# A hybrid state-space and attention layer on one core: other steps for the state-space units inside the attention loop

## The chip, the core and the metric

One NeuronCore of one Trainium2 chip runs the whole layer in one launch. Its engines are TensorE (matrix products, "PE" in the profile, "PEld" for its weight loads), VectorE ("DVE"), ScalarE ("ACT"), GpSimd ("POOL") and SyncE ("SP", which here only issues DMAs). Products are written to PSUM banks, and ScalarE and VectorE read them from there. The metric is device time in microseconds, median of the runs.

## The reference

For 2048 tokens of width 1024, one layer of a hybrid trunk, in float32:

```python
h = rmsnorm(x, norm_mix_g)
proj = h @ w_in
u_ssm, q, k, v = ...                      # 512 columns each
y_ssm = s5_mixer(u_ssm, ...)              # diagonal complex state-space layer, 32 groups of 16, GELU and a GLU
y_att = chunked_attention(q, k, v, rel_bias)   # 8 heads of 64; own chunk of 64 frames and 8 chunks before it
mixed = concatenate([rmsnorm(y_ssm, g1), rmsnorm(y_att, g2)])
x = x + mixed @ w_out
h2 = rmsnorm(x, norm_ffn_g)
x = x + (silu(h2 @ w_gate) * (h2 @ w_up)) @ w_down
return rmsnorm(x, norm_final_g)
```

The state-space layer is a recurrence over time with a constant complex factor per state: `s[t] = a * s[t-1] + B u[t]`, `y[t] = Re(C s[t]) + D u[t]`.

## The kernel before

**Stages.** First the columns of the state-space input are projected (`u_phase`), then comes the attention stage (`att_phase`), in which the rest of the projection, attention and the state-space recurrence are interleaved; then the mixing and output projection (`mix_phase`), the gated feed-forward (`gate_up_phase`) and the down projection (`down_phase`). Products are written in parts of high and low precision, so that one product of two operands is three matmuls (`mm3`).

**The attention loop.** `att_phase` goes through 128 steps: 4 blocks of 512 tokens, in each 4 pairs of heads, 2 heads, 4 groups of 128 queries. One step writes, in the order given by `ORDER` ("s", "p", "t", "f"): the scores of this step (tile `sc`, PSUM, one buffer; VectorE adds the bias and takes the minimum `mn`, L963, ScalarE takes the exponential, L966), then at the end of a head the product with the values (`pv_head`, or `pv_scale` one step later, both in PSUM tile `pj`, two buffers), then the transposes of the probabilities of two steps before (tile `pt`, PSUM, one buffer; ScalarE copies the high part `pth`, L982, and VectorE the low part `ptl`, L983), and last "f": a share of the filler work. At the steps whose number is 24 or 25 in a block (24, 25, 56, 57, 88, 89) the order is "p", "t", "f", "s". Here step n begins in the trace with its `sc` products; what the text calls f(n) is the filler work of step n, so f(88) stands ahead of the scores of step 88, and f(79) behind step 79's and directly ahead of step 80's.

**The filler work** is a list of `Unit` objects: a generator, a number n of parts, a first step s0 and an end step s1, and `pre`. `Unit.advance(s)` is called for each unit of the list, in the order of the list, at each step. From step s0 - pre on it runs the first part (the loads). From s0 on it runs so many parts that they are spread evenly up to s1; `mid=(m, ...)` asks for one part more from step s0 - m on. The projections of q, k and v of the next block (tile `pf`) and its hidden state (`hT_unit`: scaled by VectorE, L793, split in a high part by ScalarE, L813, and a low part by VectorE, L815) are in the list first. A block change is at steps 24, 56 and 88: there the last projection of one block ends and the first of the next one begins (`CUT[0]` is -8 and `CUT[-1]` is 24).

**The state-space units.** At the end of the list stand, for b = 0 to 7, `ssm_front(b)` and then `ssm_back(b)`, so that within a step the back of unit b comes ahead of the front of unit b + 1. The text counts them from one: the first unit is b = 0, the seventh b = 6.

- `ssm_front`: one part that loads the input `U` (for the second unit, b = 1, into two tiles that attention has left free) and the matrix `Bst` (L606); then two parts, one for each half q of the unit's groups: products with `Bst` into a `pj` bank and four ScalarE copies into tile `X` (L630); then 22 parts in which GpSimd scans over time (L644 to L647, then L655 and L656), and at the end issues four DMAs that carry the states from `X` to tile `XG` (L678). Each instruction of the scan works on both halves of `X`. `X`, `XG`, `Bst`, `Tm` and `Vm` have one buffer each.
- `ssm_back`: loads `Tm` (L687) and `Vm` (L692); then for each half q two products with `Tm` and `U` and two with `Vm` and `XG` into a `pj` bank, which ScalarE copies back to `U` (L701); then a store of `U` to `y` (L703).

TensorE's instructions keep the order in which the program writes them (`k.ta` and `k.te` pin every matmul). On the other engines the framework that builds the kernel chooses the order within what the data allow.

**Where the units stand** (lines 709 to 711, and line 1066, one long line):

```python
ST = 2, 10
SX = 4, 19, 33, 45, 56, 68, 80, 92
SY = 20, 34, 46, 57, 69, 81, 93, 105
...
units.append(Unit(ssm_front(...), SSM_F, SX[b], SX[b] + 9, SX[b] - 2 if b == 0 else 4, light=SL))
units.append(Unit(ssm_back(k, sp, psum, S, b), SSM_B, SY[b], SY[b] + 2, 6, light=SL))
```

`SSM_F` is 25 parts over 9 steps: at step SX[b] the front runs both halves and the first step of the scan. `SSM_B` is 4 parts over 2 steps: at step SY[b] the back runs both halves. So, from the second unit on, each back stands one step behind the front of the next unit: fronts at 33, 45, 56, 68, 80, 92 and backs of the unit before at 34, 46, 57, 69, 81, 93.

## Time and profile before

| | |
|---|---|
| median of 3 runs | 2189.12 us (2188.07 to 2189.96) |
| profiled execution, its time | 2187.64 us |
| its span in the trace | 2185.5 us |
| TensorE busy | 2144.4 us, 98% of the span |
| VectorE, ScalarE, GpSimd busy | 1535.0, 1008.2, 378.7 us |
| attention steps 0 to 127, first scores to last | 126.3 to 665.5 us |
| scores of step 21, 46, 47 | from 208.7, 309.7, 319.4 us |
| scores of step 69, 79, 80 | from 415.0, 458.0, 460.6 us |
| scores of step 88, 92 | from 499.7, 519.1 us |

The time of an execution holds some 2 us beside the span of the trace. In the rows below the first number is the start of an instruction (or of a merged run of equal ones, "x8") in us from the span's start, the second its duration; in square brackets stands how long the engine was idle before it and what released it. In a table of windows the columns are the window, its length, the busy time of each engine with its number of instructions, the granted TensorE clock as a share of full speed (PEclk), the busy share of the DMA engines and GB/s. Matmul durations overlap, so the pace of TensorE is read from one start to the next.

### The profile page before, as it was taken

What the parts mean: (1) busy time and instruction counts of PE and PEld (TensorE: products, weight loads), DVE (VectorE), ACT (ScalarE), POOL (GpSimd) and SP (SyncE); (2) the same over time, 40 slices, a digit from 0 to 9 for tenths busy, and PEclk for the clock granted to TensorE, in tenths of its full rate; (3) what the DMA queues carried; (4) which work ended last, traced back from release to release, by engine and by line L of the source; (5) the groups of instructions that cost most, each with busy time, mean ns of one, the idle gap of its engine ahead of it and who ended that gap; (6) DMA issues with size and microseconds to landing.
All of it is one profiled execution on the core that took longest, in us unless ns stands there. A gap on an engine that the chain in (4) does not pass through costs nothing.

```text
span 2185.5 us, 30150 instructions
## 1 busy us (share of the span) xinstructions
PE 2144.4 (98%) x10606; PEld 1810.5 (83%) x10606; DVE 1535.0 (70%) x2680; ACT 1008.2 (46%) x1697; POOL 378.7 (17%) x849
## 2 busy tenths in 40 slices
PE   8998999999998999999999999999999999999998
PEld 7787898898887888888888888888888888888887
DVE  8767566666567667766776769766665587688785
ACT  7356466555586621533333345333333443353322
POOL 3367777676310000000000000000000100000000
PEclk9999999999999999999999999999999999999999
DMA  9788877965745346834554757555433476575552
GB/s 337 229 285 266 295 231 247 306 218 167 211 145 178 111 144 206 286 108 148 173 184 139 246 197 278 189 174 193 158 124 98 153 291 221 192 252 182 202 212 78
DMA packets 197592, 440.12 MB, mean 201 GB/s; under 512 B 20225, under 2 KB 37681, under 8 KB 190337
## 3 DMA queue, kind: packets, MB, share of 16 engines
q1 hardware_dynamic: 188816, 410.34, 56.1%
q0 software_dynamic: 8624, 27.86, 4.1%
q8 instruction: 83, 1.36, 0.3%
q14 instruction: 69, 0.56, 0.1%
HBM read 294.72 MB, written 135.29 MB: 197 GB/s over the span
## 4 chain that ended last, share of the span: by engine, by line
PE 89%; DVE 5%; DMA 2%; ACT 2%; issue 2%; SPq 0%; POOL 0%; DVEq 0%; ACTq 0%
PE X L83 22%; PE ps L83 22%; PE Y L83 11%; PE pf L83 10%; PE big L83 9%; PE W L83 5%; PE pj L83 4%; PE pt L86 2%; PE sc L83 2%; DVE ptl L983 1%; DVE w L182 1%; DVE lo L815 0%; DMA w<-wss 0%; DMA xt<-in_xp 0%; PE pp L83 0%
## 5 line engine op out<-in xcount | busy, mean ns | idle before, releaser
L83 PE MATMUL X<-hi,c 128*128 128x512 f32 x1408 | 448.9, 389 | 0.0
L83 PE MATMUL ps<-hd,hd 128*128 128x512 f32 (+1 forms) x1920 | 428.0, 384 | 0.0
L83 PEld LDWEIGHTS ps<-hd,hd 128*128 128x128 f32 x1920 | 353.4, 188 | 70.9 <-DVE hd L182 0.3
L83 PEld LDWEIGHTS X<-hi,c 128*128 128x128 f32 x1408 | 264.3, 188 | 55.2 <-DVE c L182 0.4
L83 PE MATMUL X<-lo,c 128*128 128x512 f32 x704 | 273.9, 389 | 0.0
L182 ACT CAST hd<-hd 128x1536 fp32r<-128x1536 f32 (+2 forms) x114 | 148.0, 1309 | 226.3 <-DMA hd<-hq 165.1
L83 PE MATMUL Y<-hi,c 128*128 128x512 f32 x696 | 222.2, 389 | 0.0
L182 DVE TENSOR_TENSOR hd<-hd 128x1536 fp32r<-128x1536 f32 (+2 forms) x114 | 174.8, 1539 | 32.3 <-ACT hd L182 31.9
L182 DVE TENSOR_TENSOR c<-S,c 128x512 fp32r<-128x512 f32 x175 | 120.2, 687 | 98.7 <-ACT c L182 98.4
L1620 ACT COPY u<-X 128x512 f32<-128x512 f32 x132 | 77.5, 587 | 191.6 <-PE X L83 191.5
L83 PE MATMUL big<-m,woh 128*128 128x512 f32 x512 | 160.1, 394 | 0.0
L1830 DVE TENSOR_TENSOR acc<-acc,ps 128x512 f32<-128x512 f32 x196 | 130.4, 681 | 42.1 <-PE ps L83 41.7
L182 ACT CAST c<-S 128x512 fp32r<-128x512 f32 x175 | 108.6, 622 | 107.5 <-PE Y L83 58.0
L83 PEld LDWEIGHTS X<-lo,c 128*128 128x128 f32 x704 | 132.2, 188 | 27.3
L83 PEld LDWEIGHTS Y<-hi,c 128*128 128x128 f32 x696 | 130.7, 188 | 27.3 <-DVE u L1624 0.2
L182 ACT CAST c<-raw 128x512 fp32r<-128x512 f32 x130 | 81.0, 623 | 152.2 <-PE Y L83 72.0
L83 PE MATMUL pf<-hi,w 128*128 128x512 f32 x416 | 148.2, 409 | 0.0
L1808 POOL DMA_DIRECT2D hd<-hq x4 | 2.5, 628 | 810.9 <-PE X L83 810.1
L83 PE MATMUL Y<-lo,c 128*128 128x512 f32 x348 | 135.4, 389 | 0.0
L983 DVE TENSOR_TENSOR ptl<-pt,pth 128x640 fp32r<-128x640 f32 (+3 forms) x152 | 98.1, 645 | 45.1 <-ACT pth L982 41.2
L966 ACT ACTIVATE s<-s,mn 128x640 f32<-128x640 f32 (+4 forms) x128 | 97.9, 765 | 50.7 <-DVE mn L963 47.8
L982 ACT CAST pth<-pt 128x640 fp32r<-128x640 f32 (+3 forms) x152 | 83.8, 551 | 76.3 <-PE pt L86 70.8
(514 smaller groups left out, 4280.6 us busy)
## 6 DMA issues: line engine op xcount, KB each, us to landing
w<-wss SPq DMA_DIRECT2D x36, 1024.0 KB, 6.9
hq<-g SPq DMA_DIRECT2D x140, 256.0 KB, 2.1
hd<-hq SPq DMA_DIRECT2D x35, 768.0 KB, 4.4
hd<-wc SPq DMA_DIRECT2D x35, 768.0 KB, 5.9
raw<-in_w_up SPq DMA_DIRECT2D x44, 512.0 KB, 4.0
raw<-in_w_gate SPq DMA_DIRECT2D x43, 512.0 KB, 3.7
wc<-px SPq DMA_DIRECT2D x66, 256.0 KB, 3.0
wss<-w SPq DMA_DIRECT2D x12, 1024.0 KB, 6.6
```

The lines of the kernel that those rows point to most:

```text
L83: return self.tc.keep_in_program_order(self.tc.nc.tensor.matmul(*a, **b))
L86: return self.tc.keep_in_program_order(self.tc.nc.tensor.transpose(*a, **b))
L182: return nc.scalar.copy(hi, raw), nc.vector.tensor_tensor(lo, raw, f32(hi), op=ALU.subtract)
L966: nc.scalar.activation(s[:, :nk], s[:, :nk], AF.Exp, bias=mn[:], scale=-1.0, accum_out=sums[sb, pr][:, hh, qp : qp + 1])
L982: k.high = nc.scalar.copy(pth[:, a:b, qp, :], pt[:, a:b, :]).ins
L983: k.low = nc.vector.tensor_tensor(ptl[:, a:b, qp, :], pt[:, a:b, :], f32(pth[:, a:b, qp, :]), op=ALU.subtract).ins
L1620: self.kept = nc.scalar.copy(u[:], ps[:]).ins
L1808: k.ahead = nc.gpsimd.dma_start(f32(lo[:, d]), src[d].rearrange("g p c -> p g c")).ins
L1830: V.tensor_tensor(a, a, ps[:], op=ALU.add)
```

## The change

```diff
 ST = 2, 10
-SX = 4, 19, 33, 45, 56, 68, 80, 92
-SY = 20, 34, 46, 57, 69, 81, 93, 105
+SX = 4, 19, 33, 45, 56, 67, 78, 92
+SY = 24, 34, 46, 57, 68, 79, 88, 105
+SPRE = SX[0] - 2, 9, 4, 4, 4, 4, 4, 4
...
-                units.append(Unit(qk_unit(sb, 0), QK_N, g0 + C[0], g0 + C[1], 3, light=LIGHT))
+                units.append(Unit(qk_unit(sb, 0), QK_N, g0 + C[0], g0 + C[1], 5 if sb == 1 else 3, light=LIGHT))
...
-            units.append(Unit(ssm_front(...), SSM_F, SX[b], SX[b] + 9, SX[b] - 2 if b == 0 else 4, light=SL))
+            units.append(Unit(ssm_front(...), SSM_F, SX[b] + 1, SX[b] + 9, SPRE[b] + 1, light=SL, mid=(1,)))
```

What it does:

1. **Front in two steps, for all eight units.** With `s0 = SX[b] + 1` and `mid=(1,)` the front's first half (products and four copies) is written at step SX[b], and the second half at step SX[b] + 1, where the scan begins. The scan still ends at step SX[b] + 8.
2. **Fronts sooner.** The sixth unit (b = 5) from step 68 to 67, the seventh (b = 6) from 80 to 78; their loads, four steps ahead, move with them.
3. **Backs moved.** The first unit from step 20 to 24 and the seventh from 93 to 88, both block changes; the fifth from 69 to 68 and the sixth from 81 to 79, so that they stay one step behind the next front. Their loads, six steps ahead, move with them.
4. **Two loads sooner.** The inputs of the second unit's front are loaded from step 10 instead of 15 (`SPRE[1]` is 9), and the weights of the second block's first q and k projection (`qk_unit(1, 0)`) from step 19 instead of 21.

## The prediction

> **What bounds the kernel now.** I read the page first: busy shares, slices, chain.

> ```profile
> PE 2144.4 (98%) x10606; PEld 1810.5 (83%) x10606; DVE 1535.0 (70%) x2680; ACT 1008.2 (46%) x1697; POOL 378.7 (17%) x849
> ...
> PE 89%; DVE 5%; DMA 2%; ACT 2%; issue 2%; SPq 0%; POOL 0%; DVEq 0%; ACTq 0%
> ```

> TensorE carries the time. The change leaves its products as they are, so it can win only pauses of TensorE and stretches with a low clock, and lose only by new ones. Next come TensorE's waits in the loop (120 to 590 us) and a table of windows around two block changes.

> ```profile
> engine line waited for: us in total, times, longest us
> PE pt L86 <- DVE ptl L983: 7.4, 10, 1.3
> PE sc L83 <- DVE mn L963: 6.6, 6, 1.9
> ...
> 195.70:232.10 36.40, 32.56 (x155) 26.10 (x154) 25.55 (x56) 21.27 (x57) 24.70 (x53) 0.95 0.87 288
> 498.00:520.00 22.00, 17.61 (x91) 14.73 (x90) 16.48 (x25) 11.09 (x21) 9.61 (x11) 0.92 0.77 238
> ```

> TensorE mostly waits for VectorE. Around the first block change (195.7 to 232.1) it idles 36.40 - 32.56 = 3.84 us, and the clock of 0.95 costs 0.05 x 36.4 = 1.8 us more: 5.7 us to win at most. Around the third it is 22.00 - 17.61 = 4.4 us and 0.08 x 22 = 1.8 us: 6.2 us. Nothing else that the change touches has as much to give.

> **First block change: back of the first unit from f(20) to f(24), second unit's loads sooner.** Here are VectorE's pauses (three rows) and TensorE's rows behind them.

> ```profile
> 203.24 0.29 DVE L963 CUSTOM_DVE_ANT_0 s<-sc,nbb 128x128 f32<-128x128 f32 x1 [4.16 <-PE sc L83]
> ...
> 206.12 0.29 DVE L983 TENSOR_TENSOR ptl<-pt,pth 128x128 fp32r<-128x128 f32 x1 [1.26 <-ACT pth L982]
> ...
> 209.36 0.43 DVE L963 CUSTOM_DVE_ANT_0 s<-sc,nbb 128x256 f32<-128x256 f32 x1 [1.14 <-PE sc L83]
> ```

> ```profile
> 201.06 1.10 PE L83 MATMUL pj<-hi0x,Bst 128*128 128x256 f32 x4 [1.32 <-DMA Bst<-bsts]
> ...
> 205.47 0.59 PE L83 MATMUL pj<-U,Tm 128*128 128x256 f32 x2
> 205.90 0.59 PE L83 MATMUL pj<-XG,Vm 128*128 128x256 f32 x2
> ...
> 208.73 0.47 PE L83 MATMUL sc<-k,q2h 128*128 128x256 f32 x1
> ```

> TensorE first waits 1.32 us for `Bst`, then spends 208.73 - 205.47 = 3.3 us on the back, and VectorE, fed by it, idles 4.16 + 1.26 + 1.14 = 6.6 us; afterwards it is late with its splits, and TensorE waits for it. With the loads five steps sooner the first wait goes, hidden under projection work; if SP's queue held them back again it would cost the same 1.3 us. The back at f(24) fills the pauses there instead of starving VectorE at f(20). The gain lies between 1.3 us (the load alone) and 5.7 us (all of it). VectorE's 6.6 us of idle time exceed the loss, but its work in the stretch is dense afterwards, so I take **-4.5 us**, nearer to the upper end. Splitting the copies (eight of 0.38 us, row below) into two fours shortens ScalarE's longest block by 1.5 us and fills a pause elsewhere: at nothing, within 0.5 us. The sooner weights of the second block's first q and k shift an SP issue by two steps; no wait for them stands in the rows: nothing.

> **What the split does to the scan.** The second half of a front is now written in the step of the previous unit's back, and behind it in the list. The scan needs both halves. From the second unit's back on, its start therefore moves behind that back. And `XG` must land before the back's `Vm` products, which stand in TensorE's fixed order: whatever is behind them (scores, transposes, everything) waits. So I follow the chain: second half ready, copies, scan, four DMAs, landing.

> ```profile
> 464.99 3.03 ACT L630 COPY X<-pj 64x256 f32<-64x256 f32 x8 [1.54 <-issue]
> ...
> 468.10 0.48 POOL L644 TENSOR_TENSOR st<-X,a 128x128 f32<-128x128 f32 x1 [9.27 <-ACT X L630]
> ```

> ```profile
> L678 POOL DMA_DIRECT2D XG<-X x4: 602/617/632, 501.9 to 507.6; - x4
> ...
> DMA to landing us min/median/max: 3.6/4.0/4.8
> ```

> These are the seventh unit: the scan takes 507.6 - 468.10 = 39.5 us to its fourth DMA, which lands some 4.0 us later. Ahead of it stand four copies (4 x 0.38 = 1.5) and the end of the product (0.25). The whole chain is 1.75 + 39.5 + 4.0 = **45.3 us** from the end of f(SX + 1). The fourth and sixth unit:

> ```profile
> 312.42 0.50 POOL L644 TENSOR_TENSOR st<-X,a 128x128 f32<-128x128 f32 x1 [10.46 <-ACT X L630]
> ...
> L678 POOL DMA_DIRECT2D XG<-X x4: 599/618/635, 345.9 to 351.3; - x4
> ...
> DMA to landing us min/median/max: 2.4/3.8/4.4
> ```

> ```profile
> 417.71 0.49 POOL L644 TENSOR_TENSOR st<-X,a 128x128 f32<-128x128 f32 x1 [17.15 <-ACT X L630]
> ...
> L678 POOL DMA_DIRECT2D XG<-X x4: 599/616/632, 452.9 to 458.2; - x4
> ...
> DMA to landing us min/median/max: 2.3/2.9/3.4
> ```

> That is 1.75 + 38.9 + 3.8 = 44.4 and 1.75 + 40.5 + 2.9 = 45.1 us. Against it stands TensorE's own time between the same points:

> ```profile
> 319.44 0.50 PE L83 MATMUL sc<-k,q2h 128*128 128x320 f32 x1
> ...
> 361.09 0.59 PE L83 MATMUL pj<-U,Tm 128*128 128x256 f32 x2
> ...
> 364.36 0.50 PE L83 MATMUL sc<-k,q2h 128*128 128x320 f32 x1
> ...
> 413.49 1.89 PE L83 MATMUL pj<-U,Bst 128*128 128x256 f32 x8
> 415.02 0.50 PE L83 MATMUL sc<-k,q2h 128*128 128x320 f32 x1
> ...
> 460.60 0.31 PE L83 MATMUL sc<-k,q2h 128*128 128x320 f32 x1
> ...
> 463.88 1.89 PE L83 MATMUL pj<-rsn,Bst 128*128 128x256 f32 x8
> 465.42 0.50 PE L83 MATMUL sc<-k,q2h 128*128 128x320 f32 x1
> ...
> 499.73 0.31 PE L83 MATMUL sc<-k,q2h 128*128 128x320 f32 x1
> ```

> A front's products take 465.42 - 463.88 = 1.5 us, half of them 0.75.
> - *Back of the fourth unit, f(57).* From the end of f(46) (319.44) to its first product (361.09) it is 41.65 us; half a front moves behind it, -0.75; its second group, which needs the fourth DMA, comes 2 x 0.43 us later (205.47 to 205.90): 41.8. Chain 44.4: a wait of 2.6. The next front's first copies may not write `X` before the DMAs have read it, and they hold one of two `pj` banks that the back's second half wants: 1.5 us of copies against 0.4 of products left, 1.1 more. **+3.7** (with landings from 2.4 up to 8.4, below: 1.2 to 8.3).
> - *Back of the sixth, f(79).* From 415.02 to 460.60 it is 45.6 us; the fifth unit's back now lies ahead, -3.3, half a front lies inside, +0.75, the two groups +0.85: 43.9. Chain 45.1: 1.2, and 1.1 for the bank. **+2.3** (0 to 7.8).
> - *Back of the seventh, f(88).* From 460.60 to 499.73 it is 39.1 us; without the front (-1.5) and the back (-3.3) that now lie earlier, and with the two groups (+0.85), 35.2. Chain 45.3: **+10.1** (7.9 with the fourth unit's scan and 2.4 of landing, 14.5 with a landing of 8.4). The wait exceeds every bound of the pauses that it could fill.

> ```profile
> L678 POOL DMA_DIRECT2D XG<-X x4: 599/616/632, 243.5 to 248.9; - x4
> ...
> DMA to landing us min/median/max: 5.9/7.4/8.4
> ```

> The back at f(68) has 413.49 - 364.36 + 0.75 + 0.85 = 50.7 us against a chain of some 45, and those at f(34) and f(46) stand 14 and 12 steps behind their scans' starts instead of 11: no wait, unless landings are slow. While TensorE stands at f(88), VectorE and ScalarE finish the splits that made it wait there: of the 6.2 us I take back **-5.5**. Moving a back or a front within TensorE's order is the same work in another place: nothing. The loads that move with them (`U`, `Bst`, `Tm`, `Vm`, `SP`'s queue) still stand four or six steps ahead, and the first unit's store, now at step 25, three steps ahead of the load that needs its tile: nothing, with the 1.3 us of `Bst` as the price where SP's queue is held.

> **The clock after a pause.**

> ```profile
> 386.50:391.50 5.00, 4.90 (x40) 4.89 (x41) 2.19 (x5) 2.12 (x5) 4.37 (x12) 1.00 1.03 336
> 226.40:232.00 5.60, 5.41 (x19) 4.27 (x20) 2.62 (x8) 3.02 (x9) 4.66 (x24) 0.70 0.80 266
> 515.70:519.00 3.30, 3.30 (x11) 2.65 (x10) 2.80 (x4) 1.68 (x4) 0.00 (x0) 0.59 0.55 129
> ```

> Behind clusters of pauses the clock was 0.70 over 5.6 us and 0.59 over 3.3 us, a loss of 1.7 and 1.4 us; in the first window, behind a lone pause, it stayed at 1.00. The 10 us at f(88) will cost such a stretch: **+1.5**. For the two shorter waits I take 0 and keep 3 us for the range. [...]

> **Sum.** -4.5 + 3.7 + 2.3 + 10.1 - 5.5 + 1.5 = **+7.6 us** on the profiled 2187.64 us, 2195.2; the median of the runs lies 1.5 us above that execution: **2196.7 us**. Everything after the loop is 98% TensorE and shifts with it. 0.2% of the time, 4.4 us, is about what a measurement can tell from no change.

> **The rivals.**
> - *The chain is a little shorter.* All three waits hang on it, so 2.5 us less per unit makes them 1.2, 0 and 7.6: the sum falls to +0.3, **2189.4 us**. For it: the sixth unit's landing of 2.9 us. Against: the 8.4 us above.
> - *The wait only replaces the old pauses (faster).* Place: f(88). If scan and landing come to 5.5 us less, the waits are 0, 0 and 4.6, all 6.2 us come back, and the clock stays up: -4.5 + 4.6 - 6.2 = -6.1, **2183.0 us**. The sum turns to a gain from about 3 us less on, to one over 0.2% from about 5. For it: TensorE and VectorE stand still while GpSimd finishes, and 3.9 us of the seventh scan's window are not busy (row below). Against: three scans within 38.9 to 40.5 us.
> - *The queues carry the wait on.* `X` copies stand in ScalarE's queue until the DMAs have landed, and SP's queue waits for backs (row below), with weights behind it. Two us more at four backs: **2204.7 us**.

> ```profile
> 468.00:508.30 40.30, 36.45 (x88) 1.00 0.70 225
> ...
> SPq L687 <- PE pj L83: 29.2, 6, 8.9
> ```

> **How the numbers follow.** Forecast 0.50, shorter chain 0.20, replaced pauses 0.16, queues 0.14. Slower by over 0.2%: 0.50 + 0.14 = 0.64; within: 0.20; faster: 0.16. The forecast alone spans 2193.5 to 2202. The range reaches down past the shorter chain to 2185.5, which leaves out most of the faster case, and up to 2206.5, which takes in the queues and leaves out landings of 8 us.

> **What would show it.** In TensorE's waits of the changed kernel: `pj <- DMA XG` with a longest wait near 10 us just ahead of step 88's scores, and smaller ones at f(57) and f(79); no `pj <- DMA Bst` near 200 us; the scans starting some 5 to 9 us later against the steps; scores at 500 to 520 us without waits for `mn`, under a low clock at first. I am wrong if the `Vm` products of f(88) find `XG` landed, or if the scan starts before the previous back's products.

## The result, and the profile after

| | before | changed |
|---|---|---|
| median of 4 runs | 2188.60 us (2187.61 to 2189.96) | 2210.91 us (2208.78 to 2214.77) |
| ratio, 95% interval | | 1.0110 (1.0095 to 1.0124) |
| profiled execution, its span | 2187.64, 2185.5 us | 2212.01, 2210.0 us |

The change makes the kernel slower by 22.3 us. The forecast was 2196.7, slower by 7.6: the direction is right, the size three times too small, and the time lies above the range. One of the four executions of the kernel "fronts first", told below, took 4379 us and is left out of its median and its ratio. First the page of the changed kernel: busy time of each engine, then the shares of the chain that ended last.

```profile
PE 2151.9 (97%) x10606; PEld 1812.9 (82%) x10606; DVE 1536.4 (70%) x2680; ACT 1006.8 (46%) x1697; POOL 381.6 (17%) x849
...
PE 75%; POOL 12%; issue 6%; DVE 3%; ACT 1%; DMA 1%; SPq 0%; DVEq 0%; POOLq 0%; ACTq 0%
```

The work is the same in number, and TensorE's busy time is 7.5 us longer (a low clock counts as busy: from 228.28 to 231.69 us before, TensorE reads 3.41 of 3.41 us busy at a granted clock of 0.50). The chain tells more: GpSimd, which had no share of it before, has 12%, with the scan's lines in it. 12% of 2210 us are some 265 us: the scan now sets the pace of about half of the attention loop. TensorE's waits in the loop (120 to 620 us; what it waited for, us in total, times, longest):

```profile
PE pt L86 <- DVE ptl L984: 9.8, 11, 2.3
PE pj L83 <- DMA XG<-X: 8.8, 1, 8.8
PE pj L83 <- ACT X L630: 4.2, 4, 2.7
PE pj L83 <- issue: 3.2, 1, 3.2
PE sc L83 <- DVE mn L964: 3.1, 3, 1.9
```

The wait for `Bst` is gone, and the waits for `mn` have halved (6.6 to 3.1). New are the 8.8 us for `XG`, the 4.2 for `X` copies, 3.2 put down to "issue", and a longer one for `ptl`.

To see where the time comes from, I read the start of a step's scores in both traces and take how much a stretch of steps has grown. The columns after the forecast are the changed kernel and six experiments told below (us; the last row is the start of step 127 against that of before).

| steps | forecast | changed | split alone | whole fronts | both halves late | fronts first | fourth whole | seventh back at 93 |
|---|---|---|---|---|---|---|---|---|
| 19 to 27 | -4.5 | -3.6 | -2.3 | -2.7 | -2.6 | -3.6 | -3.6 | -3.6 |
| 27 to 31 | 0 | +1.6 | +0.1 | +3.9 | +2.4 | +1.7 | +2.4 | +1.5 |
| 45 to 47 | 0 | +4.3 | +3.8 | 0.0 | +1.2 | +1.2 | +8.4 | +4.7 |
| 55 to 58 | +3.7 | +6.5 | +5.8 | 0.0 | +7.9 | +4.6 | +0.6 | +5.4 |
| 66 to 70 | 0 | +2.5 | 0.0 | +0.2 | +0.3 | +1.4 | +2.1 | +1.5 |
| 78 to 82 | +2.3 | +5.7 | +1.1 | +0.2 | +5.9 | +1.9 | +5.4 | +5.8 |
| 87 to 94 | +6.1 | +5.9 | -2.8 | +4.6 | +6.5 | +5.8 | +6.9 | -0.5 |
| step 127 | +7.6 | +22.3 | +5.8 | +4.5 | +21.7 | +11.4 | +20.2 | +13.7 |

What lies behind step 127 differs by -1.5 to +4 us from one execution to another, so the loop is read by itself. Two of the experiments have the code of before up to step 52; they begin step 31 at -0.8 and +0.9 us, because their `Bst` wait was 0.2 and 2.3 us in place of 1.3. So a start of a step up to there is good to about 1 us, but a single stretch is not: in these two, of one code, 19 to 27 reads -2.7 and +0.8, because one of them had lost 1.9 us ahead of step 19. A stretch with the clock at half speed (3.41 us at 0.50 before), which costs up to 0.50 x 3.41 = 1.7 us, lies at 228 us before, at 176 in the one and at 202 in the other. The row 27 to 31 lies between +1.5 and +5.2 in the kernels below that have the changed kernel's loads there, and 87 to 94 between -1.2 and +1.5 in five that are there as before.

**f(88).** The forecast was right here. TensorE's rows at 516 and 525 us, with the clock over that stretch (columns as in the tables of windows before), and GpSimd's DMAs of the seventh unit:

```profile
515.95 0.59 PE L83 MATMUL pj<-rsn,Tm 128*128 128x256 f32 x2
525.29 1.22 PE L83 MATMUL pj<-XG,Vm 128*128 128x256 f32 x2 [8.76 <-DMA XG<-X]
```

```profile
515.70:530.00 14.30, 5.54 (x19) 4.30 (x17) 3.04 (x4) 0.81 (x2) 7.88 (x10) 0.76 0.53 173
```

```profile
L678 POOL DMA_DIRECT2D XG<-X x4: 599/616/632, 518.2 to 523.5; - x4
...
DMA to landing us min/median/max: 2.3/3.5/4.6
```

The back's `Tm` products are done at once, the `Vm` products wait 8.76 us until the scan, which goes on to 523.5, has been copied over. The products behind the wait take up to twice as long (1.06 where the same pair takes 0.59 later); the clock, 0.65 from 525.29 to 530.00 us, costs 0.35 x 4.7 = 1.6. The row is +5.9, so about 8.8 + 1.6 - 5.9 = 4.5 us of the old pauses came back, where the forecast had 5.5.

**f(57).** Here the forecast saw a wait for `XG`. The trace shows none:

```profile
361.29 0.41 PE L83 MATMUL sc<-k,q2h 128*128 128x320 f32 x1 [0.68 <-DVE k L861]
364.15 0.81 PE L86 MATMUL pt<-ident,s 128*128 128x128 f32 x5 [2.30 <-DVE ptl L984]
...
370.63 0.70 PE L83 MATMUL pj<-U,Tm 128*128 128x256 f32 x2 [0.34 <-ACT X L630]
...
373.15 1.13 PE L83 MATMUL pj<-rsn,Bst 128*128 128x256 f32 x4 [0.53 <-ACT U L701]
```

TensorE waits 3.0 us for VectorE, and then runs on a low clock:

```profile
364.00:370.00 6.00, 5.85 (x22) 4.76 (x22) 1.55 (x5) 0.90 (x3) 0.22 (x1) 0.72 0.85 263
```

That is 0.28 x 6 = 1.7 us more. VectorE is late because the low parts of the next hidden state (L816, L815 before) take longer. VectorE before, then VectorE and GpSimd in the changed kernel, in the same place:

```profile
353.72 1.29 DVE L815 TENSOR_TENSOR lo<-raw,hi 128x512 fp32r<-128x512 f32 x2
```

```profile
357.32 3.19 DVE L816 TENSOR_TENSOR lo<-raw,hi 128x512 fp32r<-128x512 f32 x2
...
361.99 1.25 DVE L816 TENSOR_TENSOR lo<-raw,hi 128x512 fp32r<-128x512 f32 x1
```

```profile
356.93 1.39 POOL L655 TENSOR_TENSOR fx<-X,a 128x434 f32<-128x434 f32 x1
...
360.51 1.06 POOL L655 TENSOR_TENSOR fx<-X,a 128x434 f32<-128x434 f32 x1
361.65 1.04 POOL L656 TENSOR_TENSOR X<-X,fx 128x434 f32<-128x434 f32 x1
```

Two low parts take 3.19 us where they took 1.29. In that time GpSimd, whose scan began later, is still in its last pass (L655, L656). The pass ends at 362.7 us; before it ended at 350.3, and step 55 is only 3.1 us late, so it ends some 9 us later against the steps. The forecast did not look at what VectorE does there.

**f(46) and f(79).** The third unit's back, forecast at nothing, waits for a bank; the sixth unit's back waits for `XG` ("issue" is where the trace names nothing; the `Vm` products follow the landing). TensorE and ScalarE at f(46), the DMAs of the third unit, TensorE at f(79):

```profile
316.22 0.70 PE L83 MATMUL pj<-rsn,Tm 128*128 128x256 f32 x2 [2.71 <-ACT X L630]
```

```profile
314.67 1.50 ACT L630 COPY X<-pj 64x256 f32<-64x256 f32 x4 [8.41 <-DMA XG<-X]
```

```profile
L678 POOL DMA_DIRECT2D XG<-X x4: 599/616/635, 302.6 to 307.9; - x4
...
DMA to landing us min/median/max: 3.9/6.6/8.8
```

```profile
475.89 0.67 PE L83 MATMUL pj<-XG,Vm 128*128 128x256 f32 x2 [3.22 <-issue]
```

The third unit's four transfers land 3.9 to 8.8 us after their issue; the last one, issued at 307.94 us, lands at 314.49, after 6.6 us (before, the last one of this unit took 4.2). Until then the fourth unit's first half may not be copied into `X`: its four copies wait 8.41 us on ScalarE and hold one of the two `pj` banks that the third unit's back needs. TensorE asked for it at 313.5. With a landing of 4.2 us the copies would have freed it at some 313.8, by my estimate: the slow landing makes this wait. A low clock follows, 0.28 x 6 = 1.7 us again:

```profile
316.00:322.00 6.00, 5.78 (x19) 4.81 (x20) 1.84 (x3) 3.45 (x8) 0.00 (x0) 0.72 0.00 0
```

### The profile page after: what moved, and what is told of

The parts are those of the page before. It is cut to its first block, busy times and chain, and to the rows that moved or that the text cites. A ratio compares the mean times of both kernels' runs of the same rounds, so it can differ in the third digit from the quotient of the medians.

```text
span 2210.0 us, 30145 instructions
## 1 busy us (share of the span) xinstructions
PE 2151.9 (97%) x10606; PEld 1812.9 (82%) x10606; DVE 1536.4 (70%) x2680; ACT 1006.8 (46%) x1697; POOL 381.6 (17%) x849
## 4 chain that ended last, share of the span: by engine, by line
PE 75%; POOL 12%; issue 6%; DVE 3%; ACT 1%; DMA 1%; SPq 0%; DVEq 0%; POOLq 0%; ACTq 0%
PE ps L83 21%; PE X L83 21%; PE Y L83 11%; PE big L83 9%; PE W L83 5%; PE pf L83 4%; POOL X L647 2%; POOL st L644 2%; POOL X L646 2%; POOL X L656 2%; POOL fx L655 2%; POOL st L645 2%; PE pj L83 1%; PE pt L86 1%; PE sc L83 1%
## 5 line engine op out<-in xcount | busy, mean ns | idle before, releaser
L83 PE MATMUL X<-hi,c 128*128 128x512 f32 x1408 | 448.9, 389 | 0.0
L83 PE MATMUL ps<-hd,hd 128*128 128x512 f32 (+1 forms) x1920 | 428.0, 384 | 0.0
L83 PEld LDWEIGHTS ps<-hd,hd 128*128 128x128 f32 x1920 | 353.3, 188 | 71.0 <-DVE hd L182 0.3
L83 PEld LDWEIGHTS X<-hi,c 128*128 128x128 f32 x1408 | 264.3, 188 | 55.2 <-DVE c L182 0.4
L83 PE MATMUL X<-lo,c 128*128 128x512 f32 x704 | 273.9, 389 | 0.0
L83 PE MATMUL Y<-hi,c 128*128 128x512 f32 x696 | 222.2, 389 | 0.2 <-DVE u L1625 0.2
L83 PE MATMUL big<-m,woh 128*128 128x512 f32 x512 | 161.3, 397 | 0.0
L83 PEld LDWEIGHTS X<-lo,c 128*128 128x128 f32 x704 | 132.2, 188 | 27.4
L83 PEld LDWEIGHTS Y<-hi,c 128*128 128x128 f32 x696 | 130.7, 188 | 27.7 <-DVE u L1625 0.6
L83 PE MATMUL pf<-hi,w 128*128 128x512 f32 x416 | 148.7, 410 | 0.0
L83 PE MATMUL Y<-lo,c 128*128 128x512 f32 x348 | 135.4, 389 | 0.0
L83 PE MATMUL W<-hi,c 128*128 128x512 f32 x352 | 115.5, 389 | 0.0
```

Source lines behind the costliest of these rows:

```text
L83: return self.tc.keep_in_program_order(self.tc.nc.tensor.matmul(*a, **b))
```

## The experiments

Three theories stood at the start. Q: ScalarE's early copies, waiting for the DMAs, block its queue and hold a bank, and this is what costs. C: the scan starts later against the back that needs it, and that alone costs. S: the split is harmless, and the moved backs cost.

**The split alone.** The kernel before, with only the split:

```diff
-... SSM_F, SX[b], SX[b] + 9, SX[b] - 2 if b == 0 else 4, light=SL))
+... SSM_F, SX[b] + 1, SX[b] + 9, (SX[b] - 2 if b == 0 else 4) + 1, light=SL, mid=(1,)))
```

> The kernel before with the front in two steps and nothing else of the change. Theory Q (queue: the first half's copies stand in ScalarE's queue until the previous unit's XG DMAs have read X, and pth, exp and yt behind them wait, so TensorE starves): ScalarE waits of 4 us and more for 'DMA XG<-X' at several fronts; TensorE loses some 11 us in all, 2200 us. Theory C (chain alone: TensorE waits only where Vm products arrive before XG has landed): with the old steps only f(46) and f(57) are short, 3 to 4 us in all, 2192 us. Rival S (the split is harmless, all the loss comes from the backs and fronts moved): 2188 to 2189 us.

Measured: 2194.37 us against 2187.45, ratio 1.0037 (1.0024 to 1.0051). S falls. The time lies between what C and Q asked. By the table, f(46) and f(57) cost as in the changed kernel; f(79) and the third block change don't. At the third block change this kernel even gains 2.8 us; 1.7 of them are the low stretch of the clock at 515 us before, which this execution does not have, and for the rest no cause is shown.

**Everything but the split.** The changed kernel with whole fronts:

```diff
-... SSM_F, SX[b] + 1, SX[b] + 9, SPRE[b] + 1, light=SL, mid=(1,)))
+... SSM_F, SX[b], SX[b] + 9, SPRE[b], light=SL))
```

> The change without the split: all moved fronts, backs and loads, both halves of a front at step SX as before. Q and C: scans start ahead of the previous back again, so only f(88) waits, some 5 us, against 4 to 5 us of old pauses there that go, and 4.4 us won at the first block change: 2184 to 2187 us, at most one ScalarE wait for XG over 2 us. Rival S: 2205 us or more.

Measured: 2191.19 against 2187.45, ratio 1.0016 (1.0008 to 1.0025). That is above the 2184 to 2187 that Q and C asked, and far below the 2205 of S. Without the split the rows of f(46), f(57), f(68) and f(79) are within 0.2 of nothing, so within this change the split costs 18 to 20 us. What is left is f(88), 4.6 us with a wait of 6.4 for `XG`, and the weights at f(30), which eat the gain of the first block change.

**Both halves late.** The changed kernel, but no half ahead: both are written at step SX + 1, behind the previous unit's back, so that no copy waits for `XG`.

```diff
-... SPRE[b] + 1, light=SL, mid=(1,)))
+... SPRE[b] + 1, light=SL))
```

> The changed kernel with both halves of each front written at step SX + 1, behind the previous unit's back, so that the scan starts no sooner than in the changed kernel but no copies stand in ScalarE's queue a step ahead. Q: the ScalarE waits of 5 to 10 us for XG go, TensorE loses at f(46) and f(57) nearly nothing more: 2200 us or less. C: scan starts the same or 1.5 us later, all waits as long or longer: 2211 to 2216 us.

Measured: 2210.24 against 2187.45, ratio 1.0103 (1.0088 to 1.0118), the time of the changed kernel. Q falls as the cause of the whole: no copy waits for `XG` in ScalarE's queue, f(46) and f(68) shrink by 5.3 us together, but f(57), f(79) and f(88) grow by 2.2 and the steps 19 to 31 by 1.8, and the loop ends only 0.6 us sooner. The time is just below the 2211 to 2216 that C asked. TensorE's waits for `XG` there:

```profile
PE pj L83 <- DMA XG<-X: 10.0, 3, 8.8
```

**Fronts first in the list.** The changed kernel with all fronts ahead of all backs in the list of units, so that the second half is written ahead of the previous unit's back.

```diff
         for b in range(NG // GB):
             units.append(Unit(ssm_front(...
+        for b in range(NG // GB):
             units.append(Unit(ssm_back(...
```

> The changed kernel, with all fronts ahead of all backs in the list of units: in the step that both share, the second half of a front is then written ahead of the previous unit's back. Theory 'chain': the scans start a back's length sooner, 3.3 us of products and about 2 us of bank waits, so the waits at f(57), f(79) and f(88) shrink by 2 to 4 us each, and the whole by 6 to 10: 2201 to 2205. Rival 'order holds nothing': X may be written only when the previous unit's four DMAs have read it, and the second half now stands ahead of the back's first group and makes that wait too; the time stays within 3 us of the changed kernel, or gets worse.

Measured: 2200.55 against 2187.89, ratio 1.0052 (1.0033 to 1.0070). As C asks, f(46), f(57) and f(79) shrink by 1.9 to 3.8 us each. f(88) stays, with a wait of 8.80 us: the seventh scan begins 35.8 us ahead of that back's first product (469.34 to 505.12) instead of 32.3 (483.67 to 515.95), but its transfers take a median of 6.1 us to land where they took 3.5, and the 3.5 us of lead are gone.

```profile
L678 POOL DMA_DIRECT2D XG<-X x4: 602/618/635, 503.6 to 509.3; - x4
...
DMA to landing us min/median/max: 5.3/6.1/7.2
```

**The fourth front whole.** The changed kernel, only the fourth unit's front (b = 3) in one step:

```diff
-... SSM_F, SX[b] + 1, SX[b] + 9, SPRE[b] + 1, light=SL, mid=(1,)))
+... SSM_F, SX[b] + (b != 3), SX[b] + 9, SPRE[b] + (b != 3), light=SL, mid=(1,) * (b != 3)))
```

> The changed kernel, but the fourth unit's front is not split: both halves at step 45, ahead of the third unit's back. Theory 'late scan': the scan then starts some 9 us sooner against the steps, its last passes and DMAs are over before the block change, VectorE's low parts there take 0.7 instead of 1.2 to 1.7 us; the 4 us at f(46) and the 7 us at f(57) with its low clock both go: 2199 to 2202. Rival 'pauses carried': most of what shows at f(57) comes from the earlier split fronts or from the second half written behind the third back at step 57 itself; then no more than the 4 us of f(46) goes: 2206 to 2208.

Measured: 2208.79 against 2187.89, ratio 1.0092 (1.0077 to 1.0107). The time is just above the rival's 2206 to 2208. The theory is right at f(57), 6.5 to 0.6 us, and wrong at f(46), which doubles. With a whole front both `pj` banks hold products that may not be copied until the third unit's late transfers have landed, and the product with the values behind them has no bank (TensorE, then ScalarE's wait):

```profile
315.46 0.79 PE L83 MATMUL pj<-pth,v 128*128 128x512 f32 x1 [6.64 <-ACT X L630]
```

```profile
ACT X L630 <- DMA XG<-X: 8.0, 1, 8.0
```

One late scan was enough here: it delayed the next front, whole (ScalarE's wait of 8.0 us) or split (8.41).

**Spare GpSimd work.** The kernel before with eight more GpSimd instructions behind the fourth unit's DMAs, to a scratch tile:

```diff
+    if b == 3:
+        for _ in range(4):
+            t = k.t(p, "fx", ...)
+            pw = a8[:, 0, qs, 0:7].unsqueeze(2).to_broadcast(...)
+            eng.tensor_tensor(t, pw, pw, op=ALU.mult)
+            eng.tensor_tensor(t, t, pw, op=ALU.add)
```

> The kernel before with eight more GpSimd instructions (of the size of the scan's last passes, 128x434, written to a scratch tile that nobody reads) behind the fourth unit's DMAs: GpSimd is then busy from 352 to some 361 us, across VectorE's five low parts of the second block change, and nothing else is moved. Theory 'shared access': those low parts take 1.2 to 1.7 instead of 0.7 us, VectorE comes 3 us late, TensorE waits for VectorE at the block change and its clock falls behind it: 3 to 6 us, 2190.5 to 2193.5. Rival 'no collision': the low parts stay at 0.7 us; the fifth unit's scan starts at most 0.5 us later, and the time is that of before within 1 us.

Measured: 2188.16 against 2187.89, ratio 1.0007 (0.9996 to 1.0018). The time is the rival's, that of before. The collision is there all the same, and its price is smaller than I expected:

```profile
354.48 2.85 DVE L821 TENSOR_TENSOR lo<-raw,hi 128x512 fp32r<-128x512 f32 x2
```

```profile
354.05 1.42 POOL L684 TENSOR_TENSOR fx<-fx,a 128x434 f32<-128x434 f32 x1
```

```profile
360.66 0.77 PE L86 MATMUL pt<-ident,s 128*128 128x128 f32 x5 [1.26 <-DVE ptl L989]
```

The low parts take 2.85 in place of 1.29 us, GpSimd's own instructions up to 1.42 in place of 1.06, and steps 55 to 58 grow by 1.5 us, with the clock at 1.00. Less of VectorE's work was hit than in the changed kernel, and one pause of 1.26 us did not bring the clock down.

**The control: writes in place of reads.** The same place, but twenty writes of zeros to the scratch tile; then the changed kernel, in which the fourth unit's last pass is replaced by such writes, its DMAs behind them.

```diff
+    if b == 3:
+        for _ in range(20):
+            t = k.t(p, "fx", ...)
+            eng.memset(t[:], 0.0)
```

> The kernel before with twenty writes of zeros to a scratch tile behind the fourth unit's DMAs, beside the low parts of the second block change, in place of the eight spare instructions with two inputs. Theory 'collision' (two readers of SBUF): all low parts there take 0.7 us, TensorE's wait for VectorE of 1.3 us does not come, and step 57 begins within 0.3 us of before. Rival 'length': they take 0.9 to 1.4 us as beside the spare instructions with two inputs, and 1 to 1.5 us are lost at step 56 and 57.

> The changed kernel, but the fourth unit leaves out the last pass of its scan: in place of its eight GpSimd instructions with two inputs stand twenty writes of zeros to a scratch tile, of about the same length together (some 9 us), and the four DMAs stand behind them. GpSimd is busy as long and XG lands no sooner, but GpSimd reads nothing. [...] Theory 'collision': VectorE's low parts at the second block change take 0.7 us again, the 3 us of TensorE's waits for VectorE and the low clock at f(56) and f(57) go, and a wait for XG of 2 to 5 us shows at f(57) instead, as the chain asks; f(57) costs 3 to 5 us, and the whole is 2207 to 2209. Rival 'length': the low parts are slow because GpSimd is busy at all; then they stay at 1.2 to 1.7 us, and f(57) costs some 7 us as in the changed kernel.

In the first (one execution, so only its rows are read) GpSimd is busy with writes from 354.29 to 364.85 us, and steps 55 to 58 grow by 0.0 us:

```profile
354.29 10.56 POOL L682 MEMSET fx<- 128x448 f32 x20
```

```profile
355.79 1.28 DVE L819 TENSOR_TENSOR lo<-raw,hi 128x512 fp32r<-128x512 f32 x2
```

So in these rows GpSimd's being busy does not by itself slow VectorE, whose instruction with two operands in SBUF took 2.85 us for two in a row beside GpSimd's `tensor_tensor`, which reads SBUF, and 1.28 beside its writes of zeros. That the reading makes the difference is my inference from these two kernels.

The second measured 2211.54 against 2187.14, ratio 1.0108 (1.0091 to 1.0125), 2 us and more over its expectation, and steps 55 to 58 grow by 9.4 us, not by 3 to 5. (Another 3.6 us of its distance from the changed kernel come at steps 27 to 31, where its code is the same.) But the rival falls, for VectorE is in time again, and what its delay had covered comes out:

```profile
358.79 1.28 DVE L825 TENSOR_TENSOR lo<-raw,hi 128x512 fp32r<-128x512 f32 x2
```

```profile
363.16 0.77 PE L86 MATMUL pt<-ident,s 128*128 128x128 f32 x5 [0.31 <-DVE ptl L993]
...
372.92 1.19 PE L83 MATMUL pj<-XG,Vm 128*128 128x256 f32 x2 [6.48 <-DMA XG<-X]
```

The wait for `XG` that the forecast had placed at f(57) is there, 6.48 us of it. The last DMA ends 1.6 us later against step 56 than in the changed kernel, so there the wait would have been some 4.9 us, less if the first two transfers, which stand together with the others here, had landed well ahead; the forecast was 2.6. Either way the late scan is paid for: by VectorE's delay, or by the wait behind it.

**The seventh back at step 93.** The changed kernel with `SY[6]` = 93:

> The changed kernel with the seventh unit's back at f(93) again, one step behind the next front as the other backs stand. Theory 'chain': the 8.8 us wait for XG and the 3 us behind it at f(88) go, the pauses of the third block change (some 6 us) come back, and the other waits stay: 2203 to 2206. Rival 'the wait moves on': the eighth unit's split front at 92 and 93 now stands around the back as at the other units, and takes 4 us or more there: 2207 to 2211.

Measured: 2206.73 against 2186.56, ratio 1.0090 (1.0072 to 1.0108). The time lies between the theory's 2203 to 2206 and the rival's 2207 to 2211, but the rows are the theory's: the 5.9 us of steps 87 to 94 become -0.5, and the wait doesn't move on. The 8.8 us wait is gone from the list, the 3.2 of f(79) stays:

```profile
PE pj L83 <- issue: 3.3, 1, 3.3
```

**Whole fronts and the seventh back at 93.** Both together:

> The changed kernel with whole fronts and the seventh unit's back at f(93): what is left is the first unit's back at f(24), two fronts and two backs one or two steps sooner, and the loads. Theory 'chain': no scan starts later against its back than before, so no wait is left but that for w at f(30), and the time is that of before within 1 us: 2187 to 2188.5. Rival: the sooner sixth and seventh unit cost something themselves, because their scans and copies meet other work; then 2190 or more.

Measured: 2186.74 against 2186.56, ratio 0.9994 (0.9985 to 1.0003): as C asks, no back waits for `XG` and nothing is lost. The sooner sixth and seventh unit cost nothing that can be told by themselves.

**The first block change by itself.** Three kernels, each the kernel before with the first unit's back at f(24) and the second unit's input sooner: with the weights of the first q and k sooner too; without; and with them and the weights of the first v two steps sooner (`v_unit(1, 0)`, `pre` 5 in place of 3).

> The kernel before with the first unit's back at step 24 and the two loads sooner, nothing else. All theories: the 4.3 us that the changed kernel was ahead by at step 27 stay: 2184 to 2185 us. If that lead came from the split at the second unit's front, only the 1.3 us of Bst go: 2187.5 us.

> The kernel before with only the first unit's back at f(24) and the second unit's input sooner; the weights of the second block's first q and k stay where they were. Theory 'SP queue': with the sooner weights the two weight loads of f(30) stood behind both k loads in SP's queue, and the 2.3 us won by step 27 were given back there. Left in place, both stand ahead of the second k load, so the wait for w at f(30) is below 1 us and the 2 to 3 us stay: 2184.5 to 2185.5. Rival 'buffer': the weights are late because the back now holds something else up at the block change; the wait of some 2 us at f(30) stays and the time is that of before within 1 us.

> The kernel before with the first unit's back at f(24), the second unit's input and the weights of the second block's first q and k sooner, and one thing more: the weights of its first v are asked for two steps sooner too, so that the first of the two loads stands ahead of the second k load in SP's queue. Theory 'SP queue': the wait for w at f(30) falls from 2.4 us to under 0.7 and the 2 to 3 us won by step 27 stay to the end: 2185 to 2186, a ratio of 0.9988. Rival: the second of the two loads is late as well, or the load only delays the k load behind it; the lead is lost and the time is that of before within 1 us.

Measured: 2187.96 against 2187.45, ratio 1.0007 (0.9997 to 1.0017); 2187.84 against 2187.89, 0.9999 (0.9989 to 1.0009); 2186.18 against 2186.56, 0.9995 (0.9985 to 1.0004). None can be told from before, though the theory asked 2184 to 2185 of the first and 2184.5 to 2185.5 of the second. The traces say why. SP's queue before, in the first and in the third (issue, duration):

```profile
221.90 0.42 SPq L829 DMA_DIRECT2D k<-ks  x1
226.01 0.33 SPq L772 DMA_DIRECT2D w<-wss  x1
232.75 0.33 SPq L829 DMA_DIRECT2D k<-ks  x1
236.68 0.44 SPq L772 DMA_DIRECT2D w<-wss  x1
```

```profile
220.26 0.40 SPq L829 DMA_DIRECT2D k<-ks  x1
223.56 0.32 SPq L703 DMA_DIRECT2D y<-U  x1
230.43 0.32 SPq L829 DMA_DIRECT2D k<-ks  x1
235.14 1.18 SPq L772 DMA_DIRECT2D w<-wss  x2
```

```profile
219.86 0.38 SPq L829 DMA_DIRECT2D k<-ks  x1
221.58 0.32 SPq L772 DMA_DIRECT2D w<-wss  x1
230.04 0.32 SPq L829 DMA_DIRECT2D k<-ks  x1
```

In the first, both weight loads for f(30) stand behind the second k load, which waits until 230.43; one had gone at 226.01 before. TensorE waits up to 1.4 us at a time for `w`, and the 2.6 us won by step 27 are lost by step 31. In the second the weights of f(24) are late instead (a wait of 1.83 us at 218.84), and nothing is won. In the third the first load stands ahead again, the loss from 27 to 31 is 0.9, and the loop ends 3.1 us ahead of before. That is 0.14% of the time, the traced execution was the fastest of its twelve (2182.82), and the interval holds no change: no kernel here is shown to beat the kernel before.

## Why the prediction was right in direction and wrong in size

The step that failed most is "The back at f(68) ... and those at f(34) and f(46) ...: no wait, unless landings are slow". It put these backs at nothing, on landings of 2.9 to 4.0 us; landings of 6.6 us made most of the +4.3 at f(46), the largest single miss, and the +2.5 at f(68) stands behind such landings too. Besides, the wait at f(79) was sized too small, and two costs were not looked for: VectorE beside the late scan, and the order in SP's queue.

- **The mechanism of the split: right.** The scans start behind the previous back, and their end is late for the next one. Split alone, whole fronts, fronts first and the seventh back at 93 each move the rows that they should.
- **f(34), f(46) and f(68), nothing: failed at the last two.** The condition came true: behind the third unit the last transfer took 6.6 us, behind the fifth too. The range was drawn to leave out landings of 8 us, and in the changed kernel 4 of the 8 units have one above 7. The late landing holds up the next front's copies, and these hold a bank: +4.3 at f(46), 2.7 of it the wait and 1.7 a low clock, and +2.5 at f(68), with two waits for banks (0.53 and 1.24 us) at full clock.
- **f(79), +2.3: size.** From the start of step 69 (429.1) to the place of the first `Vm` products (472.6) TensorE needed 43.5, near the 43.9 that I had worked out. The chain took 2.0 to the scan, 41.4 for it (to 472.5) and 3.4 more until the products ran at 475.89: 46.8 for 45.1. With the pauses for banks behind it (0.6 and 0.9) the row is +5.7; not each part of it has a row.
- **f(57), +3.7: the named wait was not the one.** VectorE was late first, by a collision with GpSimd that no step of the prediction looked for, and its delay covered the wait for `XG`: 3.0 us of waits, 1.7 of low clock, 0.9 for banks, of +6.5. (The lower ends of the ranges given there and at f(79), 1.2 and 0, also leave out the 1.1 us for the bank.)
- **f(88) and the third block change, +6.1 together: right, with some luck.** Measured +5.9; the wait was 8.8 for 10.1, but about 4.5 us of the old pauses came back and not 5.5, and the two misses cancel.
- **First block change, -4.5: the way is right, the size in part luck.** -3.6 by step 27, and the wait for `Bst` (1.3) is gone. 1.7 us of it are the low stretch at 228 us, which one kernel with the code of before didn't have there either; and the split alone, with the first back where it was, is 1.7 us ahead at step 27. What the back itself brings is not shown. "The sooner weights ... no wait for them stands in the rows: nothing" failed: they changed the order in SP's queue, and the next weights came late, +1.6 by step 31, and up to +5.2 in the other kernels with these loads.
- **"For the two shorter waits I take 0" (clock): failed** at f(57), by 1.7 us. At f(79) the clock stayed at 1.00, but that was luck: in the kernel with the seventh back at 93 it fell there to 0.50 behind a wait of 3.34 us (see the end).
- **The rivals.** "The queues carry the wait on" (2204.7) had the nearest time, but its mechanism isn't what decides: with no copies waiting in ScalarE's queue the kernel takes as long. Copies do hold a bank at f(46).

The terms that were too small, 1.6 + 4.3 + 2.8 + 2.5 + 3.4 = 14.6 us, lead from the 7.6 forecast to 22.2; the loop measured 22.3, and what the other rows miss by, up to 1 us each, about cancels.

## What to carry to other kernels

When a chain on an idle engine has as little slack as one step, forecast each of its deadlines with the slowest landing that the trace shows, since here one late landing, 6.6 us at the third unit where it had been 4.2, held the buffer `X` and one of the two banks (TensorE waited 2.71 us), and with them the next chain. Ask also what the late engine now runs beside: moved by 9 us, GpSimd's pass fell on VectorE's low parts, two of which took 3.19 us where they had taken 1.29. And a load asked for sooner was not free here, where SP's queue issues all loads (+1.6 us from step 27 to 31): read which load it passes, and what then stands behind a waiting one.

## What the runs showed of the hardware that I had not expected

```profile
470.56:473.97 3.41, 2.11 (x17) 1.70 (x15) 0.56 (x2) 0.00 (x0) 2.23 (x3) 1.00 0.57 152
473.97:477.39 3.42, 1.50 (x6) 1.06 (x6) 0.00 (x0) 0.90 (x3) 0.00 (x0) 1.00 0.34 88
477.39:480.80 3.41, 2.03 (x9) 1.44 (x8) 1.45 (x3) 3.37 (x9) 0.00 (x0) 1.00 0.07 14
```

```profile
470.05:473.46 3.41, 0.26 (x2) 0.00 (x0) 0.00 (x0) 0.00 (x0) 0.96 (x2) 1.00 0.62 164
473.46:476.87 3.41, 3.22 (x8) 2.63 (x9) 0.41 (x1) 2.61 (x6) 0.00 (x0) 0.50 0.00 0
```
